# A hybrid-attention encoder layer: keys loaded once with queries turned on chip, value products one group later, and another order of loads and passes in the merge

## The chip, the cores and the metric

The kernel runs on one core of a Trainium2 chip. The metric is the device time of one execution in microseconds (us). The engines of the core are named as in the profile: PE is TensorE (matmuls; PEld is its weight load), DVE is VectorE, ACT is ScalarE, POOL is GpSimd, and SP is SyncE, which here issues nearly all the DMAs. "SPq" marks an instruction of SP's queue that issues a DMA. Each engine works its own queue of instructions in order; semaphores hold an instruction until what it needs is done.

## The reference

One layer on a sequence of 2048 tokens of width 1024, all in float32:

```python
h = rms_norm(x, norm_mix)
q_a, k_a, v_a, q_b, k_b, v_b, g_a, g_b = split(h @ w_in)   # 4352 columns
y_a = windowed_gqa(q_a, k_a, v_a, sink)       # |t-s| <= 128, 8 heads, 2 key/value heads
y_b = neighborhood_attn(q_b, k_b, v_b, rpb)   # 8 heads on a grid of 32 x 64, 8 x 16 neighbours
merged = sigmoid(g_a) * (y_a @ w_proj_a) + sigmoid(g_b) * (y_b @ w_proj_b)
x = x + merged @ w_out
x = x + square(relu(rms_norm(x, norm_mlp) @ w_up)) @ w_down
out = rms_norm(x, norm_final)
```

In the first attention ("A") a block of 128 queries sees the 384 keys around it, with a bias that falls with distance and one sink logit per head. In the second ("B") a tile of queries, 8 grid rows by 16 columns, sees a patch of keys with a learned bias.

## The kernel before, in words

**Arithmetic.** Products of float32 numbers are made from two rounded parts, hi and lo: `a*b = ah*bh + ah*bl + al*bh`, three matmuls (`mm3`, `mm3s`, lines 201 and 278). To split a tile, ACT rounds it (`A.copy`, L275 in `split`) and DVE subtracts (L276). Large products use a seven-product block scheme (Strassen's kind), which is why operands are sums of blocks, numbered 1 to 7.

**Stages, in order of time.** The input projection runs to about 500 us of the span, attention A from there to about 800, attention B to about 1115, the merge (gated projections, then `merged @ w_out`) to about 1390, the up projection to about 1990 and the down projection to the end.

**Scores.** Heads are 64 wide, so hi and lo of a query fill the 128 rows of the array: a query tile is `[qh; ql]`. The keys lie in SBUF twice: plane 0 is `[kh; kl]` and plane 1 is `[kl; kh]`, and the two matmuls of a score (L850 and L851 in A, L1070 in B) use the same query tile against the two planes, which gives all four products. A load of keys is three DMAs: the whole of plane 0 (L830, L1047) and the two halves of plane 1, each on 64 partitions (L831 and L832; L1048 and L1049). In A there are four such loads (`load_kv`), in B eight (`load_k`, one for each head, into two tiles in turn).

**A unit of attention.** There are 32 units of A (`attn_a`) and 32 of B (`attn_b`). A unit loads its queries (L843, L1057), makes scores into PSUM, adds bias and takes the maximum on DVE (L852, L1075), takes the exponential on ACT (L859, L1081) and scales on POOL (L863, L1086). Later it turns the probabilities 128 columns at a time on PE against the identity (L869, L1098); for each group of turned columns ACT rounds them to `ph` (L873, L1104), DVE makes the rest `pl` (L874, L1105), and two sets of matmuls with the values add to a PSUM bank (L875 and L876; L1110). At the end the two halves of the result (values' hi and lo) are added into `ya` or `yb` and stored. `drive` keeps a unit's second part two units behind its first. The values of a unit of B are a DMA of their own (L1060) into one of three tiles.

**Filling.** Beside the attention PE has other work, the gate columns of the projection (`gate_tiles`) and the projection of A's result (`proj_tiles`), dealt out by `paced` between groups of transposes.

**The merge.** It runs twice, for `m` = 0 and 1, each on half the tokens. Eight calls of `gated` load gate values (L1586) and stored projections (L1588) and make the tiles `m0` to `m3`. Then `out_products` makes seven products in the order 1, 2, 5, 6, 3, 7, 4. Each takes its weights from DRAM (`wo_d`, L1487, two loads of 1 MB) and its left operand from the `m` tiles, split by L275 and L276; weights and operands share a ring of six buffers, `pgl`. Beside them, `beside_out` loads rows of `x` (L1562), loads the next part of B's result (`load_y`, L1169), and, in the second pass, prepares the up projection (`up_start`, `up_right`, `up_left_steps`). When a block of rows is finished it is normalised (L230, L241) and turned by DVE (`turned_out`, L253), and goes to DRAM as `h2d` (L257). In the second pass, `turned_last` uses freed `m` tiles for the first of the last two row blocks and `hu` for the last.

**Memory and order.** SBUF is dealt out as stacks of pools from two sides. A pool of a later stage lies where an earlier one lay, and its first writer waits for the earlier one's last user. The order of instructions on each engine isn't that of the program text: a planner simulates the program with its own costs at build and takes, for each engine, what is ready first, with the earlier text preferred. `tc.issue_after(ins)` forbids it to put the instructions of a block ahead of `ins` on that engine's queue; it adds no semaphore. Once built, the order is fixed.

Of the kernel before, what the change touches and what calls it, by code (L numbers as in the profile page):

```python
# [8 lines left out]
F32 = mybir.dt.float32  # L9
# [83 lines left out]
def encoder_layer(ctx, tc, x, norm_mix, w_in, b_gate, sink, rpb, w_pa, w_pb, w_out,  # L93
# [179 lines left out]

    def split(src, hi, lo, eng):
        A.copy(hi, src)  # L275
        return eng.tensor_tensor(out=lo, in0=src, in1=hi.bitcast(F32), op=ALU.subtract).ins  # L276
# [532 lines left out]
    ap_ = pools(s_a, "left", ("dist", "sta", "qa", "ka1", "va1", "ya", "sa", "ph", "pl"), "a")  # L809
# [15 lines left out]
    kas = [T(ap_, [P, 2, S], F32R, f"ka{g}", 1) for g in range(2)]  # L825
    vas = [T(ap_, [P, 16, P], F32R, f"va{g}", 1) for g in range(2)]

    def load_kv(g, m):
        k, kd = kas[g][:, :, m * (S // 2) : (m + 1) * (S // 2)], ks_a[m][g]
        SY.dma_start(k[:, 0].bitcast(F32), kd)  # L830
        SY.dma_start(k[0:64, 1].bitcast(F32), kd[64:128])  # L831
        SY.dma_start(k[64:128, 1].bitcast(F32), kd[0:64])  # L832
        SY.dma_start(vas[g][:, 8 * m : 8 * m + 8].bitcast(F32), vs_a[m][g])

    def attn_a(u, g, i):
# [6 lines left out]
        q = T(ap_, [P, 4, P], F32R, "qa", 3)  # L842
        began.append(SY.dma_start(q.bitcast(F32), qs_a[g][i // 8][:, :, i % 8]).ins)  # L843
# [21 lines left out]
        po = psum("av", 2)  # L865
        for c in range(c0, c1):
# [8 lines left out]
            PE.matmul(po, v[:, i - 1 + c, :], ph, start=c == c0, stop=False)  # L875
            PE.matmul(po, v[:, i - 1 + c, :], pl, start=False, stop=c == c1 - 1)  # L876
        e = u % 2 * 64
        t = (ya if u % 4 < 2 else yb)[e : e + 64]
        A.copy(t, po[64 - e : 128 - e, :])
        V.tensor_tensor(out=t, in0=po[e : e + 64, :], in1=t, op=ALU.add)  # L880
        flush(queue=SY)
        put(y_a[g].rearrange("(h d) t -> d h t", d=64)[:, :, i * P : (i + 1) * P],
            t.rearrange("d (h q) -> d h q", h=4))
# [10 lines left out]
    def drive(units, live, last, ahead=2):  # L894

        for u in units:
            next(u)
            live.append(u)
            if len(live) > ahead:
                next(live.pop(0), None)  # L900
        while last and live:
            next(live.pop(0), None)

# [22 lines left out]
    def gate_tiles(*fs):  # L926
# [33 lines left out]
    def proj_tiles(f):  # L960
# [3 lines left out]
        for b in (0, 2):  # L964
            for i in range(2):
                z = T(wp, [P, 2, BT], F32, "z", 3)
# [20 lines left out]

    live, given = [], [0]
    units_a = [(1, i) for i in range(5)] + [(0, i) for i in range(16)] + [(1, i) for i in range(5, 16)]
    load_kv(1, 0)  # L990
    at = 0
    for n, g, m in ((4, 0, 0), (9, 0, 1), (14, 1, 1)):
        drive((attn_a(u, *units_a[u]) for u in range(at, n)), live, False)
# [4 lines left out]
    drive((attn_a(u, *units_a[u]) for u in range(14, 32)), live, True)  # L998
# [7 lines left out]
    bp = pools(s_b, "right", ("masks", "qb", "braw0", "biass", "stb", "kb0", "biasl", "braw1", "kb1"), "b")  # L1006
# [36 lines left out]
    def load_k(h):  # L1043

        k = T(bp, [P, 2, S], F32R, f"kb{h % 2}", 1)
        kd = ks_b[h // 2][h % 2]
        SY.dma_start(k[:, 0].bitcast(F32), kd)  # L1047
        SY.dma_start(k[0:64, 1].bitcast(F32), kd[64:128])  # L1048
        SY.dma_start(k[64:128, 1].bitcast(F32), kd[0:64])  # L1049
        return k  # L1050

    def attn_b(n_u, h, j, k, bias):
# [3 lines left out]
        q = T(bp, [P, 4, P], F32R, "qb", 3)  # L1056
        SY.dma_start(q.bitcast(F32), qs_b[t][e][:, :, j])  # L1057
        yield
        v = T(bp, [P, 8, P], F32R, f"vb{n_u % 3}", 1)
# [4 lines left out]
        kv = k.rearrange("p z (q f) -> p z q f", q=8)  # L1064
        s = []
        for i in range(4):
            n = B_NR[i] * w
            ps = psum("s", 3)
            for z in range(2):
                PE.matmul(ps[:, :n], q[:, i, :],  # L1070
                          kv[:, z, B_R0[i] // 4 : (B_R0[i] + B_NR[i]) // 4, 4 * B_C0[j] : 4 * (B_C0[j] + w)],
# [16 lines left out]
        flush(queue=SY)  # L1088
        po = psum("av", 2)
        first = True  # L1090
        for pair in range(4):
# [16 lines left out]
            for c, i0, ni, o in pieces:  # L1108
                for z, src in enumerate((ph, pl)):
                    PE.matmul(po[:, i0 * P : (i0 + ni) * P], v[:kp, c, :],  # L1110
                              src[:kp, o : o + ni * P], start=first, stop=(c == 7 and z == 1),
                              skip_group_check=True)
                    first = False

        at = n_u % 2 * 64
        y = yb[at : at + 64]
        A.copy(y, po[64 - at : 128 - at, :])
        V.tensor_tensor(out=y, in0=po[at : at + 64, :], in1=y, op=ALU.add)
        put(y_b[t].rearrange("(e d) (i j t) -> e d i j t", e=2, i=4, j=4)[e, :, :, j, :],
            y.rearrange("d (i t) -> d i t", i=4))  # L1120

    def all_b():
# [3 lines left out]
        for h in range(BH):  # L1126
            k = load_k(h)

            for n, j in enumerate((0, 3, 1, 2) if h == 0 else range(4)):
# [4 lines left out]
                u = attn_b(4 * h + n, h, j, k, bias)  # L1134
                next(u)
                yield u

    def ahead_of(units, n):
        ready = []
        for u in units:  # L1140
            ready.append(u)
            if len(ready) > n:
                yield ready.pop(0)
        yield from ready

# [14 lines left out]
    ring_l = [None]  # L1160
# [679 lines left out]
```

## Time and profile before

| what | us |
|---|---|
| median of 3 runs | 2623.56 |
| lowest and highest of them | 2621.88, 2627.18 |
| the profiled execution, its own time | 2622.45 |
| its span, from the first to the last instruction | 2620.7 |
| PE busy | 2551.7 |
| DVE busy | 1710.1 |
| ACT busy | 1309.0 |
| POOL busy | 354.3 |
| bytes moved | 553.21 MB, 211 GB/s over the span |

A row of the timeline gives the start and length of an instruction in us, its engine and line, what it writes and reads, and in square brackets how long the engine sat idle before it and what ended that idleness. Matmuls are pipelined: 128x512 has a length of 390 ns, but one starts about every 230 ns. A row of the table by stretches gives, for each engine, the busy us and the number of instructions, then the granted clock of PE (1.00 is full speed), the share of the DMA engines and the GB/s.

### The profile page before, as it was taken

What the parts mean: (1) busy time and instruction counts of PE and PEld (TensorE: products, weight loads), DVE (VectorE), ACT (ScalarE), POOL (GpSimd) and SP (SyncE); (2) the same over time, 40 slices, a digit from 0 to 9 for tenths busy, and PEclk for the clock granted to TensorE, in tenths of its full rate; (3) what the DMA queues carried; (4) which work ended last, traced back from release to release, by engine and by line L of the source; (5) the groups of instructions that cost most, each with busy time, mean ns of one, the idle gap of its engine ahead of it and who ended that gap; (6) DMA issues with size and microseconds to landing.
All of it is one profiled execution on the core that took longest, in us unless ns stands there. A gap on an engine that the chain in (4) does not pass through costs nothing.

```text
span 2620.7 us, 34535 instructions
## 1 busy us (share of the span) xinstructions
PE 2551.7 (97%) x11936; PEld 2123.5 (81%) x11936; DVE 1710.1 (65%) x2717; ACT 1309.0 (50%) x2345; POOL 354.3 (14%) x482
## 2 busy tenths in 40 slices
PE   8999999999999999999998999999999999999998
PEld 6788888877787887887877888888887888888887
DVE  8857677657764576665687677766655634554766
ACT  6365565557775675523246554644444332323444
POOL 1001001133446664200000000000000000000011
PEclk9999999999999999999999999999999999999999
DMA  5767878774358998797878665854428825445555
GB/s 185 224 198 251 267 241 278 217 216 113 100 162 196 214 279 231 221 325 267 303 287 251 234 219 191 293 184 145 157 101 298 308 97 185 145 147 167 185 194 168
DMA packets 347695, 553.21 MB, mean 211 GB/s; under 512 B 32072, under 2 KB 152376, under 8 KB 345344
## 3 DMA queue, kind: packets, MB, share of 16 engines
q1 hardware_dynamic: 330336, 510.48, 61.5%
q10 hardware_dynamic: 10944, 24.12, 2.5%
q0 software_dynamic: 6240, 16.40, 2.1%
q8 instruction: 94, 1.54, 0.2%
q14 instruction: 81, 0.66, 0.1%
HBM read 364.17 MB, written 186.71 MB: 210 GB/s over the span
## 4 chain that ended last, share of the span: by engine, by line
PE 75%; DMA 13%; DVE 6%; ACT 3%; SPq 2%; issue 2%; POOL 0%; DVEq 0%; POOLq 0%; ACTq 0%
PE b L280 15%; PE b L279 15%; PE b L281 15%; PE zb L281 5%; PE zb L279 5%; PE zb L280 5%; PE mm L202 2%; PE mm L204 2%; PE mm L203 2%; DMA vb<-vs_b 2%; DMA h2d<-ht 1%; PE av L1110 1%; PE pt L869 1%; DMA z<-zg 1%; PE pt L1098 1%
## 5 line engine op out<-in xcount | busy, mean ns | idle before, releaser
L280 PE MATMUL b<-dwh,dah 128*128 128x512 f32 x896 | 349.2, 390 | 0.4 <-DVE dwh L276 0.4
L281 PE MATMUL b<-dwh,dah 128*128 128x512 f32 x896 | 348.3, 390 | 0.0
L279 PE MATMUL b<-dwh,dah 128*128 128x512 f32 x896 | 339.0, 390 | 1.7 <-ACT dwh L275 1.7
L275 ACT CAST dah<-da 128x1024 fp32r<-128x1024 f32 (+1 forms) x128 | 120.8, 945 | 367.4 <-PE b L281 246.3
L279 PE MATMUL zb<-zh,zwhl 128*128 128x512 f32 x728 | 285.3, 392 | 3.7 <-ACT zc L486 1.3
L280 PE MATMUL zb<-zh,zwhl 128*128 128x512 f32 x728 | 285.6, 392 | 0.0
L281 PE MATMUL zb<-zh,zwhl 128*128 128x512 f32 x728 | 283.9, 391 | 0.8 <-DVE zwhl L276 0.8
L276 DVE TENSOR_TENSOR dah<-da,dah 128x1024 fp32r<-128x1024 f32 (+1 forms) x128 | 139.2, 1090 | 216.1 <-ACT dah L275 213.0
L279 PE MATMUL b<-ubh,uwhlb 128*128 128x512 f32 x592 | 231.5, 392 | 7.7 <-ACT uwhlb L275 4.5
L280 PE MATMUL b<-ubh,uwhlb 128*128 128x512 f32 x592 | 231.7, 391 | 0.5 <-DVE ubh L276 0.5
L281 PE MATMUL b<-ubh,uwhlb 128*128 128x512 f32 x592 | 229.8, 390 | 0.0
L279 PEld LDWEIGHTS b<-dwh,dah 128*128 128x128 f32 x896 | 168.2, 188 | 36.9 <-ACT dwh L275 2.1
L280 PEld LDWEIGHTS b<-dwh,dah 128*128 128x128 f32 x896 | 168.3, 188 | 35.6 <-DVE dwh L276 0.8
L281 PEld LDWEIGHTS b<-dwh,dah 128*128 128x128 f32 x896 | 168.3, 188 | 34.8
L272 DVE TENSOR_TENSOR uc<-b,uc 128x512 f32<-128x512 f32 x160 | 109.3, 689 | 118.1 <-PE b L281 110.8
L279 PEld LDWEIGHTS zb<-zh,zwhl 128*128 128x128 f32 x728 | 137.1, 188 | 34.2 <-ACT zc L486 2.5
L281 PEld LDWEIGHTS zb<-zh,zwhl 128*128 128x128 f32 x728 | 137.1, 188 | 28.9 <-DVE zwhl L276 1.3
L280 PEld LDWEIGHTS zb<-zh,zwhl 128*128 128x128 f32 x728 | 137.1, 188 | 27.7
L202 PE MATMUL mm<-zh,whl 128*128 128x512 f32 x368 | 157.7, 428 | 0.6 <-ACT z L463 0.6
L204 PE MATMUL mm<-zh,whl 128*128 128x512 f32 x368 | 145.5, 395 | 0.0
L203 PE MATMUL mm<-zh,whl 128*128 128x512 f32 x368 | 144.9, 394 | 0.0
L279 PEld LDWEIGHTS b<-ubh,uwhlb 128*128 128x128 f32 x592 | 111.8, 189 | 32.1 <-ACT uwhlb L275 4.9
(262 smaller groups left out, 5694.4 us busy)
## 6 DMA issues: line engine op xcount, KB each, us to landing
at<-uc SPq DMA_DIRECT2D x224, 256.0 KB, 2.1
da<-at SPq DMA_DIRECT2D x96, 512.0 KB, 3.6
dw<-in_w_down_dram SPq DMA_DIRECT2D x160, 256.0 KB, 4.4
uraw<-in_w_up_dram SPq DMA_DIRECT2D x32, 1024.0 KB, 6.0
pgl<-wo_d SPq DMA_DIRECT2D x28, 1024.0 KB, 9.8
zraw<-in_w_in_dram SPq DMA_DIRECT2D x24, 1024.0 KB
z<-zg SPq DMA_DIRECT2D x64, 256.0 KB, 4.3
qs_a<-ze SPq DMA_DIRECT2D x32, 256.0 KB, 6.0
```

Source lines behind the costliest of these rows:

```text
L202: PE.matmul(ps, lh, rh, start=first, stop=False)
L203: PE.matmul(ps, lh, rl, start=False, stop=False)
L204: PE.matmul(ps, ll, rh, start=False, stop=last)
L272: return eng.tensor_tensor(out=out, in0=a, in1=b, op=op).ins
L275: A.copy(hi, src)
L276: return eng.tensor_tensor(out=lo, in0=src, in1=hi.bitcast(F32), op=ALU.subtract).ins
L279: PE.matmul(ps, lh, rh, start=first, stop=False, skip_group_check=True)
L280: PE.matmul(ps, lh, rl, start=False, stop=False, skip_group_check=True)
L281: PE.matmul(ps, ll, rh, start=False, stop=last, skip_group_check=True)
L869: last = PE.transpose(pt[:, h * P : (h + 1) * P], s[:, h, c * P : (c + 1) * P], ident).ins
L1098: last = PE.transpose(pt[:kp, at + (i - i0) * P : at + (i - i0 + 1) * P], s[i][:, rr : rr + kp], ident)
L1110: PE.matmul(po[:, i0 * P : (i0 + ni) * P], v[:kp, c, :], src[:kp, o : o + ni * P], start=first, stop=(c == 7 and z == 1), skip_group_check ...
```

## The change

1. Keys stay once in SBUF, as `[kh; kl]`; each load is one DMA, not three. The query tile gets a second plane: ACT copies the rows 64 to 127 to rows 0 to 63, and DVE the other half (`turn_q`). The two matmuls of a score use the two planes of the query against the same keys.
2. A unit of A, like one of B, has its queries loaded one unit ahead (`ahead_of`), and the turn stands at the head of its scores.
3. The value products of a group are written in the program behind the transposes of the next group, across units too (`behind`, `result`).
4. Pools: `ya` and `va1`, and `qb`, change places; the ring `z` has four buffers, not three.
5. The merge. All four further rows of `x` come behind the loads of the weights then last asked for; so do the next part of B's result, and, in the second pass, all loads of the first four calls of `gated`. `turned_last` uses `m0` and `m1`, not `m2` and `m3`. Two passes of the up projection's right operand (`gained`) are kept behind the last rounding of the left operands so far, and so are the passes for product 3.

```diff
+    rounded = [None]
     def split(src, hi, lo, eng):
-        A.copy(hi, src)
+        rounded[0] = A.copy(hi, src).ins
...
-    ap_ = pools(s_a, "left", ("dist", "sta", "qa", "ka1", "va1", "ya", "sa", "ph", "pl"), "a")
+    ap_ = pools(s_a, "left", ("dist", "sta", "qa", "ka1", "ya", "va1", "sa", "ph", "pl"), "a")
...
+    def load_q(pl, tag, src):
+        q = T(pl, [P, 2, 4, P], F32R, tag, 3)
+        return q, SY.dma_start(q[:, 0].bitcast(F32), src).ins
+
+    def turn_q(q):
+        A.copy(q[0:64, 1], q[64:128, 0].bitcast(F32))
+        V.tensor_copy(out=q[64:128, 1], in_=q[0:64, 0].bitcast(F32))
+
-    kas = [T(ap_, [P, 2, S], F32R, f"ka{g}", 1) for g in range(2)]
+    kas = [T(ap_, [P, S], F32R, f"ka{g}", 1) for g in range(2)]
     def load_kv(g, m):
-        k, kd = kas[g][:, :, m * (S // 2) : (m + 1) * (S // 2)], ks_a[m][g]
-        SY.dma_start(k[:, 0].bitcast(F32), kd)
-        SY.dma_start(k[0:64, 1].bitcast(F32), kd[64:128])
-        SY.dma_start(k[64:128, 1].bitcast(F32), kd[0:64])
+        SY.dma_start(kas[g][:, m * (S // 2) : (m + 1) * (S // 2)].bitcast(F32), ks_a[m][g])
...
-        q = T(ap_, [P, 4, P], F32R, "qa", 3)
-        began.append(SY.dma_start(q.bitcast(F32), qs_a[g][i // 8][:, :, i % 8]).ins)
+        q, ins = load_q(ap_, "qa", qs_a[g][i // 8][:, :, i % 8])
+        began.append(ins)
+        yield
+        turn_q(q)
...
-            PE.matmul(ps[:, :n], q[:, h, :], ka[:, 0, base + lo : base + hi], start=True, stop=False)
-            PE.matmul(ps[:, :n], q[:, h, :], ka[:, 1, base + lo : base + hi], start=False, stop=True)
+            for z in range(2):
+                PE.matmul(ps[:, :n], q[:, z, h, :], ka[:, base + lo : base + hi], start=z == 0, stop=z == 1)
...
+        def result(c, ph, pl):
+            if c == c0:
+                po[0] = psum("av", 2)
+            PE.matmul(po[0], v[:, i - 1 + c, :], ph, start=c == c0, stop=False)
+            PE.matmul(po[0], v[:, i - 1 + c, :], pl, start=False, stop=c == c1 - 1)
+            if c < c1 - 1:
+                return
...
             A.copy(ph, pt)
             V.tensor_tensor(out=pl, in0=pt, in1=ph.bitcast(F32), op=ALU.subtract)
-            PE.matmul(po, v[:, i - 1 + c, :], ph, start=c == c0, stop=False)
-            PE.matmul(po, v[:, i - 1 + c, :], pl, start=False, stop=c == c1 - 1)
...
+            behind(lambda c=c, ph=ph, pl=pl: result(c, ph, pl))
+    lagged = []
+    def behind(f=None):
+        while lagged:
+            lagged.pop(0)()
+        if f:
+            lagged.append(f)
...
-                    zs[f] = T(wp, [P, 2, BT], F32, "z", 3)
+                    zs[f] = T(wp, [P, 2, BT], F32, "z", 4)
...
+    def ahead_of(units, n):
+        ready = []
+        for u in units:
+            next(u)
+            ready.append(u)
+            if len(ready) > n:
+                yield ready.pop(0)
+        yield from ready
...
-    bp = pools(s_b, "right", ("masks", "qb", "braw0", "biass", "stb", "kb0", "biasl", "braw1", "kb1"), "b")
+    bp = pools(s_b, "right", ("masks", "braw0", "biass", "stb", "kb0", "qb", "biasl", "braw1", "kb1"), "b")
...
     def load_k(h):
-        k = T(bp, [P, 2, S], F32R, f"kb{h % 2}", 1)
-        kd = ks_b[h // 2][h % 2]
-        SY.dma_start(k[:, 0].bitcast(F32), kd)
-        SY.dma_start(k[0:64, 1].bitcast(F32), kd[64:128])
-        SY.dma_start(k[64:128, 1].bitcast(F32), kd[0:64])
+        k = T(bp, [P, S], F32R, f"kb{h % 2}", 1)
+        SY.dma_start(k.bitcast(F32), ks_b[h // 2][h % 2])
...
+            behind(lambda pair=pair, pieces=pieces, ph=ph, pl=pl: result(pair, kp, pieces, ph, pl))
...
-                SY.dma_start(raw, y_b[c][:, (2 * m + j) * BT : (2 * m + j + 1) * BT])
+                with tc.issue_after(y_behind[0]) if y_behind[0] else nullcontext():
+                    SY.dma_start(raw, y_b[c][:, (2 * m + j) * BT : (2 * m + j + 1) * BT])
...
         out[4] = parts(a22, V)
+        last_left[0] = rounded[0]
...
-        gained(t, 0)
-        gained(b12, 0)
+        with tc.issue_after(last_left[0]):
+            gained(t, 0)
+            gained(b12, 0)
...
-        parts(3, b22, 1)
+        with tc.issue_after(last_left[0]):
+            parts(3, b22, 1)
...
-            SY.dma_start(w.bitcast(F32), wo_d[n][h].rearrange("k p z c -> p k z c"))
+            wo_dma[0] = SY.dma_start(w.bitcast(F32), wo_d[n][h].rearrange("k p z c -> p k z c")).ins
...
             split(src, t[:, 0], t[:, 1], V)
+            last_left[0] = rounded[0]
...
-            if n < 2:
-                rows[1].extend(x_row(m, 1, 2 * n + t) for t in range(2))
+            if n == 1:
+                with tc.issue_after(wo_dma[0]):
+                    rows[1].extend(x_row(m, 1, t) for t in range(4))
             elif m == 0 and n in (3, 5):
+                y_behind[0] = wo_dma[0]
                 state["y"] = next(loads)
-            elif m == 1:
+            elif m == 1 and n:
                 if n < 5:
                     next(loads)
                 elif n == 6:
-                    free = [T(p4x, [P, 2, 2, BT], F32, f"m{t}", 1).rearrange("p a b c -> p a (b c)") for t in (2, 3)]
+                    free = [T(p4x, [P, 2, 2, BT], F32, f"m{t}", 1).rearrange("p a b c -> p a (b c)") for t in (0, 1)]
                     turned_last(0, lambda g: free[g // 2][:, g % 2])
...
         def gated(f):
+            with tc.issue_after(wo_dma[0]) if m and f < 4 else nullcontext():
+                gated_at(f)
+        def gated_at(f):
```

The unit of B is changed like that of A; its `result` takes the pieces of a pair of chunks and ends the unit at the fourth pair.

More of the change, by code (lines that the diff above doesn't have):

```diff
@@ L997, in encoder_layer @@
     paced(fill, given, 84, 92, 12)
[L998 removed]
+    drive(all_a, live, True)
     paced(fill, given, 84, 92, 12, last=True)
@@ L1107, in attn_b @@
                 pieces.reverse()
[L1108 to L1120, printed above, removed]
+            behind(lambda pair=pair, pieces=pieces, ph=ph, pl=pl: result(pair, kp, pieces, ph, pl))
     def all_b():
```

71 lines of the change are left out of this document (41 added, 30 removed).

## The prediction

> **What bounds the kernel now.** I read the page first, then the stretches, then PE's idle moments one by one in the timeline, and last what SP and ACT did just before each.
>
> ```profile
> span 2620.7 us, 34535 instructions
> PE 2551.7 (97%) x11936; PEld 2123.5 (81%) x11936; DVE 1710.1 (65%) x2717; ACT 1309.0 (50%) x2345; POOL 354.3 (14%) x482
> ...
> core 0: us, PE busy (x) PEld busy (x) DVE busy (x) ACT busy (x) POOL busy (x), PEclk, DMA share, GB/s
> 500.00:1450.00 950.00, 907.19 (x4656) 764.98 (x4655) 623.18 (x1315) 523.46 (x1185) 298.31 (x390) 0.99 0.76 226
> 1450.00:2621.00 1171.00, 1159.04 (x5110) 959.23 (x5108) 727.08 (x942) 510.78 (x758) 14.59 (x17) 1.00 0.56 189
> ...
> 800.00:840.00 40.00, 34.19 (x184) 29.58 (x183) 17.84 (x49) 19.56 (x48) 20.59 (x25) 0.91 1.00 217
> 1034.00:1048.00 14.00, 13.64 (x72) 12.42 (x73) 7.64 (x18) 7.27 (x17) 5.64 (x6) 0.79 0.69 207
> 1195.00:1240.00 45.00, 42.78 (x182) 35.36 (x183) 24.46 (x33) 14.57 (x23) 1.67 (x3) 0.96 0.67 249
> 1285.00:1330.00 45.00, 41.58 (x176) 33.64 (x175) 36.01 (x47) 16.92 (x27) 0.00 (x0) 0.96 1.05 395
> 1410.00:1450.00 40.00, 35.65 (x148) 29.33 (x149) 29.70 (x35) 21.87 (x34) 0.00 (x0) 0.91 0.74 265
> ```
>
> PE bounds it, at 97%. The change leaves PE's work as it is: the same matmuls of the same shapes, and each had its own weight load before (as many PEld as PE). So only PE's idle time and slow clock can be won. All edits lie between 500 and 1450 us, where PE is idle for 950.00 - 907.19 = 42.8 us. The five stretches below that row show the clock granted short of 1.00; the loss is length times shortfall: 3.6, 2.9, 1.8, 1.8 and 3.6, together 13.7 us. The most that can be won is about 56 us. The idle time lies in a few places:
>
> ```profile
> 822.77 0.73 PE L1070 MATMUL s<-kb,qb 128*128 128x288 f32 x3 [2.19 <-DMA kb<-ks_b]
> 829.29 2.68 PE L1070 MATMUL s<-kb,qb 128*128 128x384 f32 x6 [3.02 <-DMA qb<-qs_b]
> 1034.36 0.55 PE L1110 MATMUL av<-phb,vb 96*128 96x256 f32 x1 [3.74 <-DMA vb<-vs_b]
> 1197.22 0.76 PE L279 MATMUL b<-pgl,pgl 128*128 128x512 f32 x1 [4.21 <-DMA pgl<-wo_d]
> 1322.28 0.50 PE L279 MATMUL b<-pgl,pgl 128*128 128x512 f32 x1 [3.42 <-ACT pgl L275]
> 1392.45 0.73 PE L279 MATMUL b<-ubh,uwhlb 128*128 128x512 f32 x2 [1.59 <-ACT ubh L275]
> 1414.35 0.79 PE L279 MATMUL b<-ubh,uwhlb 128*128 128x512 f32 x1 [4.48 <-ACT uwhlb L275]
> ...
> PE av L1110 <- DVE plb L1105: 4.8, 10, 1.0
> PE s L1070 <- DVE stb L1075: 1.6, 2, 1.2
> PE av L1110 <- ACT phb L1104: 2.3, 4, 0.9
> PE av L875 <- ACT ph L873: 2.1, 3, 1.1
> PE av L876 <- DVE pl L874: 1.4, 5, 0.4
> ```
>
> Seven gaps hold 22.7 us, three from loads in B, four in the merge; the waits of value products for `ph` and `pl` hold 4.8 + 2.3 + 2.1 + 1.4 = 10.6 us in 22 pieces. After a long gap PE is also slow: the scores at 829.29 took 2.68 us for six. The Trainium skill ("TensorE: Matmul & The Clock Gate", Part 1) has the clock halved after an idle window of about 3.4 us. By that rule the gaps of 2.19 and 3.02 us would cost no clock and the sum below would be 3.6 us smaller; the trace, with 0.91 granted between 800 and 840, does not agree.
>
> **Keys once (edit 1, the loads).**
>
> ```profile
> 804.91 17.73 DMA kb<-ks_b
> ...
> 823.28 5.87 DMA qb<-qs_b
> ...
> qb<-qs_b SPq DMA_DIRECT2D x32, 256.0 KB, 6.4
> kb<-ks_b SPq DMA_DIRECT2D x8, 1024.0 KB, 11.3
> kb<-ks_b SPq DMA_DIRECT2D x16, 512.0 KB, 12.8
> ...
> 1013.12 0.91 SPq L1047 DMA_DIRECT2D kb<-ks_b  x1
> ...
> 1019.11 0.58 SPq L1060 DMA_DIRECT2D vb<-vs_b  x1
> ```
>
> B loses 16 DMAs of 512 KB, 8 MB, where the DMA share is 1.00 (800 to 840); A loses eight smaller ones, which no gap above waits for. At 804.91 the last third of the second head's keys is issued and lands 17.73 us later, at 822.64; PE had run dry 2.19 us before, at 820.6. Half the bytes land in about half the time, near 814, before PE runs dry; the queries issued at 823.28, behind those keys on SP's queue, come forward as well. That is 2.19 + 3.02 + 3.6 of clock = 8.8 us. At 1019.11 values are issued behind 2 MB of keys (from 1013.12) and PE gets them at 1034.36; without 1 MB of those at the 207 GB/s of the row from 1034, they land 1 MB / 207 GB/s = 5 us sooner, more than the 3.74 us gap. That is 3.74 + 2.9 = 6.6 us. Together 15.4; the low end is a third, 5, if other transfers take the room. I take 12, near the upper end, since both gaps follow a load that is halved. Next late would be values again, whose slot is freed by the unit three before.
>
> **The turn (edits 1 and 2).**
>
> ```profile
> L1117 ACT COPY yb<-av 64x512 f32<-64x512 f32 x32 | 18.6, 581 | 27.9 <-DMA y_b<-yb 11.8 <-PE av L1110 6.6 <-DMA zp<-z 5.0
> L243 DVE TENSOR_SCALAR xin<-xin,st 128x1024 f32<-128x1024 f32 x4 | 3.0, 751 | 1.1 <-POOL st L234 1.1
> ```
>
> 64 turns: ACT 64 x 0.58 = 37 us; DVE 64 x 0.75/2 = 24 us (half the columns of L243's row). ACT is busy 523 and DVE 623 of the 950 us, so both have room, and the filling work of PE covers it. The new wait is one of PE's first score matmul, and of ACT and DVE for the queries' DMA: behind it on ACT stand roundings of `ph`, behind it on DVE those of `pl`, for which PE's value products wait. Lower end 0. Upper end 37 us, were each ACT copy on the path. The nearest row is the roundings: 22 late ones of about 220, 0.48 us each; for 64 turns that gives 64/220 x 10.6 = 3.1. I take 3. The Trainium skill ("SBUF — State Buffer", Who interferes with whom) says that a copy in DVE's two-port mode and a POOL instruction shut each other out for a whole instruction. No run here shows that; by it DVE's turn could wait out one of POOL's scalings, and the sum would be some 2 us larger.
>
> **The lag (edit 3).** It moves 10.6 us of waits behind at least one more group of transposes. Ends 0 (the planner had filled these places as well as it could) and 10.6. I take 7, since the waits are short (at most 1.1 us, less than a group with its six filling matmuls, which start 0.23 us apart). Next late: the values' slots are freed a group later, so their loads start later. A's and B's score waits for DVE stay.
>
> **Pools and ring (edit 4).** They move no work; a wrong neighbour would show as a load waiting for an old tile. I cost them at nothing: what hides it is the lead of one unit for queries; if gone, each costs a gap like that at 829.29.
>
> **The merge (edit 5).**
>
> ```profile
> 1179.66 4.44 SPq L1169 DMA_DIRECT2D yraw<-y_b  x4
> 1184.27 0.98 SPq L1588 DMA_DIRECT2D z<-zp  x2
> ...
> 1189.86 4.06 SPq L1487 DMA_DIRECT2D pgl<-wo_d  x4
> ...
> 1318.14 1.94 ACT L1285 ACTIVATE uraw<-uraw,g_mix 128x512 f32<-128x512 f32 x3
> ...
> 1321.20 1.98 ACT L275 CAST pgl<-m 128x1024 fp32r<-128x1024 f32 x2
> ...
> 1391.35 2.00 ACT L275 CAST ubh<-uraw 128x1024 fp32r<-128x1024 f32 x2 [2.67 <-DMA h2d<-m]
> ...
> 1407.38 1.96 ACT L546 ACTIVATE ubh<-uraw,g_mix 128x512 fp32r<-128x512 f32 x3 [2.77 <-DMA h2d<-hu]
> ...
> 1413.27 1.03 ACT L275 CAST uwhlb<-uraw 128x1024 fp32r<-128x1024 f32 x1
> ```
>
> Gap at 1197: the weights are issued at 1189.86, behind four loads of `y_b` and loads of the second pass's `gated`. Both now go behind weights: up to 4.21 + 1.8 of clock. Gap at 1322: on ACT passes of `gained` (L1285) stand ahead of the rounding of `pgl` at 1321.20; they now follow the last such rounding: up to 3.42 + 1.8. They land in ACT's later idle time (8 x 0.65 = 5.2 us). Gap at 1392: ACT waits 2.67 us for the stores from `m` before it may write `ubh`, which lies there; with `m0` and `m1` freed earlier and another neighbour, 1.59. Gap at 1414: ACT waits 2.77 us for stores from `hu` and then does product 3's passes, ahead of the rounding that PE needs (1413.27); these now stand behind it: 4.48 + 3.6. Sum 20.9. Upper end that; lower end 6, if only the last gap's idle and a part of its clock are won. I take 17, since at each gap the instruction that stood in front is the one that is moved. The price is that the second pass's first loads start only after the last weights of the first: behind them on SP stand gate values, for which DVE and then PE wait; the cover is the products still to run then.
>
> **Sum.** 12 + 7 - 3 + 17 = 33. A new order on every queue will bring a wait or two that aren't there now; I allow 6 us, one gap like those seen with its clock. Net 27. The profiled execution took 2622.45 us (span 2620.7, 1.75 around it; the median is 2623.56, 1.1 more): 2622.45 - 27 = 2595.
>
> **Rivals.**
> *Late queries stop two engines (slower).* A query tile that lands late now holds ACT and DVE, not PE alone. For: 6.4 us to landing in the middle, and one late tile at 829.29. Against: 31 of 32 came in time, and DMA gets 8 MB less. Each costs 3.02 us and half of the clock loss that two gaps share there (3.6 / 2), 4.8 in all; from six on (27 / 4.8) the gain is gone, and eight make 2595 + 8 x 4.8 = 2633.
> *The lag and the keys win little.* The planner had already put filling work there, and a slot of values freed later makes a new values gap (3.74 + 2.9). Then 5 + 0 - 3 + 17 - 6 - 6.6 = 6: 2616.
> *The merge only moves its stalls.* The second pass starts late and the loads of `x` collide with weights (395 GB/s at 1285 to 1330). Then 12 + 7 - 3 + 6 - 6 = 16: 2606.
> *It doesn't do what it says.* The planner puts the moved pieces where they were, and only the turn is new: 2622.
>
> **How the numbers follow.** My forecast 0.55 (its own range 2575 to 2605), the merge's stalls 0.17, lag and keys 0.12, nothing done 0.06, late queries 0.10. 0.2% is 5 us, about what a measurement can tell from no change. Faster: 0.55 + 0.17 + 0.09 of lag and keys = 0.81; same: the other 0.03 and 0.04 of nothing done = 0.07; slower: late queries and the last 0.02 = 0.12. The range starts at all of the upper ends, 15.4 + 10.6 + 20.9 = 47, so 2575, and ends past the unchanged time, at 2626, which leaves out late queries and little else.
>
> **What would show it.** Right: no PE gap over 1 us ended by kb, qb or vb, or by `pgl` and `uwhlb`; the granted clock at 0.98 or more in the five stretches; 8 MB fewer moved in B. The lag: waits for `ph` and `pl` under 4 us in sum. Wrong: PE waits at scores ended by the turn, with ACT or DVE idle for qb; gaps at the first products of the merge's second pass; longer waits for vb.

## The result, and the profile after

The changed kernel takes 2682.12 us (median of 4 runs, 2678.34 to 2687.74) against 2622.72 us for the kernel before in the same session. The ratio is 1.0225, with a 95% interval of 1.0203 to 1.0247: it is 2.2% slower, about 59 us, where 27 us less were predicted. The profiled execution, the slowest of the four, took 2687.74 us with a span of 2686.0.

The head of the page of the changed kernel, in the order of the one before:

```profile
span 2686.0 us, 34629 instructions
...
PE 2574.7 (96%) x11936; PEld 2128.8 (79%) x11936; DVE 1743.1 (65%) x2781; ACT 1351.5 (50%) x2409; POOL 355.8 (13%) x482
...
DMA packets 345776, 542.73 MB, mean 202 GB/s; under 512 B 31688, under 2 KB 151992, under 8 KB 344448
```

The matmuls are the same 11936. The span grew by 2686.0 - 2620.7 = 65.3 us. PE is busy 2574.7 - 2551.7 = 23.0 us longer with the same work, and idle 42.3 us longer. Part of the 23.0 is slower clock: the mean granted clock of the span is 0.987 in place of 0.994, and by the profile's record of the granted clock PE works at half clock for 51 us in place of 22, which makes some 14 us. The rest stays open. ACT and DVE got their 64 copies each and still have plenty of idle time. 10.5 MB less are moved. None of these totals says why the kernel is slower. The next view, by stretches, says where: the first table is of the changed kernel, A and B together and then the merge and the up projection, the second is of the kernel before. The stretches are bounded, within a few us, by the first scores of A, the first products of the merge and the first of the down projection; the first stretch holds 14 matmuls more in the changed kernel, some 3 us.

```profile
536.00:1183.00 647.00, 585.77 (x3169) 490.59 (x3168) 411.58 (x1041) 415.59 (x1024) 284.92 (x372) 0.97 0.54 159
1183.00:2068.00 885.00, 861.68 (x3757) 709.69 (x3756) 600.03 (x768) 421.43 (x610) 9.79 (x16) 0.99 0.65 225
```

```profile
539.00:1125.00 586.00, 560.12 (x3155) 480.73 (x3156) 377.10 (x974) 374.33 (x959) 279.66 (x364) 0.99 0.71 190
1125.00:2002.00 877.00, 859.05 (x3757) 708.28 (x3755) 600.08 (x770) 419.54 (x609) 9.77 (x16) 0.99 0.66 228
```

A and B took 586 us and now take 647, with PE idle 61 us in place of 26 and the clock at 0.97 in place of 0.99. The merge and what follows take 8 us more, where 17 less were predicted. Who waits in A and B is told by the waits of the changed kernel (engine, tile and line that waits, what ended the wait; us in total, times, longest):

```profile
ACT qb L834 <- DMA qb<-qs_b: 55.5, 28, 5.5
DVE qb L835 <- DMA qb<-qs_b: 54.7, 26, 5.6
DVE qa L835 <- DMA qa<-qs_a: 46.6, 27, 5.8
ACT qa L834 <- DMA qa<-qs_a: 20.3, 12, 4.0
...
PE s L1107 <- DVE stb L1112: 12.1, 8, 3.6
PE s L862 <- DVE sta L863: 10.1, 8, 6.5
PE av L882 <- DVE pl L901: 9.1, 12, 3.2
PE av L1133 <- DVE plb L1160: 7.7, 13, 2.2
PE av L881 <- ACT ph L900: 6.8, 7, 1.8
```

L834 and L835 are the two halves of the turn. In 93 of 128 cases (28 + 26 + 27 + 12) the half stood at the head of its engine's queue before its queries had landed, and the engine stood still: 177 us in all. No such rows exist in the profile before. PE itself hardly waits for the turn. It waits for what stands behind the turn: the passes over scores that free a bank (`sta`, `stb`) and the rounding of probabilities. One such place in the timeline:

```profile
982.39 0.56 SPq L830 DMA_DIRECT2D qb<-qs_b  x1
...
990.09 0.62 ACT L834 CAST qb<-qb 64x512 fp32r<-64x512 f32 x1 [3.01 <-DMA qb<-qs_b]
...
990.09 0.42 DVE L835 CAST qb<-qb 64x512 fp32r<-64x512 f32 x1 [5.59 <-DMA qb<-qs_b]
990.54 0.18 DVE L1120 RECIPROCAL stb<-stb 128x4 f32<-128x4 f32 x1
...
991.09 0.55 DVE L1160 TENSOR_TENSOR plb<-pt,phb 128x384 fp32r<-128x384 f32 x1
...
991.23 1.01 PE L1107 MATMUL s<-kb,qb 128*128 128x384 f32 x2 [3.62 <-DVE stb L1112]
```

The load is issued at 982.39, and both halves of its turn start at 990.09, when it has landed. DVE waits 5.59 us for it. A reciprocal and a subtraction that were ready, and the passes that free the score banks, stand behind, and PE runs dry for 3.62 us. And these queries weren't wanted yet: when the 32 loads, turns and sets of eight score matmuls of B are matched in their order in the timeline, DVE's half begins 4.8 us (median, never over 7.7) after the issue of its load, and the unit's scores begin about 18 us after that. In A it is 3.2 and about 13 us. (The queries of B's first three units are loaded and turned at the start of A already.) The planner put the turn right behind its load, and not ahead of its use.

### The profile page after: what moved, and what is told of

The parts are those of the page before. It is cut to its first block, busy times and chain, and to the rows that moved or that the text cites. A ratio compares the mean times of both kernels' runs of the same rounds, so it can differ in the third digit from the quotient of the medians.

```text
span 2686.0 us, 34629 instructions
## 1 busy us (share of the span) xinstructions
PE 2574.7 (96%) x11936; PEld 2128.8 (79%) x11936; DVE 1743.1 (65%) x2781; ACT 1351.5 (50%) x2409; POOL 355.8 (13%) x482
## 4 chain that ended last, share of the span: by engine, by line
PE 73%; DMA 11%; DVE 7%; ACT 4%; issue 3%; SPq 1%; POOL 0%; ACTq 0%; DVEq 0%; POOLq 0%
PE b L283 15%; PE b L282 15%; PE b L281 15%; PE zb L281 4%; PE zb L283 4%; PE zb L282 4%; DMA qb<-qs_b 4%; PE mm L202 2%; DMA qa<-qs_a 2%; PE mm L203 2%; PE mm L204 2%; PE av L1133 1%; PE b L202 1%; PE b L203 1%; PE b L204 1%
## 5 line engine op out<-in xcount | busy, mean ns | idle before, releaser
L202 PE MATMUL mm<-zh,whl 128*128 128x512 f32 x368 | 159.5, 434 | 10.9 <-DVE z L1007 6.4
L203 PE MATMUL mm<-zh,whl 128*128 128x512 f32 x368 | 147.5, 401 | 0.0
L204 PE MATMUL mm<-zh,whl 128*128 128x512 f32 x368 | 147.3, 400 | 0.0
```

The lines of the kernel that those rows point to most:

```text
L202: PE.matmul(ps, lh, rh, start=first, stop=False)
L203: PE.matmul(ps, lh, rl, start=False, stop=False)
L204: PE.matmul(ps, ll, rh, start=False, stop=last)
```

## The experiments

Theory T: the turn costs time by its place in the queues of ACT and DVE; the late loads hold these engines, and everything behind. Its rivals: W, the work of the 128 copies costs it; L, the lead of one unit is too short; and that the lag did it (R1 in the texts below) or that the loss is spread over the parts (R2).

**The edits apart.** Edits 1, 2 and 4 alone (keys, turn, pools):

> The kernel before with keys once, the turn, the lead of a unit and the new pools and ring alone (edits 1, 2 and 4). Theory T: the planner puts each turn directly behind its query load, the load takes longer than it was planned with, and ACT and DVE stand still before 54 of the 64 turns or so; those stalls are the whole loss of A and B, some 60 us. T expects 2670 to 2690, with ACT and DVE waits for qa and qb of over 100 us in sum. Rival R1: the lag makes the loss, by what it holds longer. R1 expects 2605 to 2630 here. Rival R2: the loss is spread over the parts. R2 expects 2635 to 2655.

```diff
 (the changed kernel, with edits 3 and 5 taken back)
-            behind(lambda c=c, ph=ph, pl=pl: result(c, ph, pl))
+            PE.matmul(po, v[:, i - 1 + c, :], ph, start=c == c0, stop=False)
+            PE.matmul(po, v[:, i - 1 + c, :], pl, start=False, stop=c == c1 - 1)
...
```

Measured: 2673.53 us, ratio 1.0182 (1.0161 to 1.0203). Its waits of the turn for the loads are 50.1 + 50.6 + 15.6 + 41.5 = 158 us. So four fifths of the loss (48 of 59 us) come with these edits.

Edit 3 alone (the lag):

> The kernel before with the lag of the value products alone (edit 3). T expects 2612 to 2625, PE's waits for ph and pl under 6 us in place of 10.6. R1 expects 2670 or more. R2 expects 2630 to 2645.

```diff
 (the kernel before, with)
-            PE.matmul(po, v[:, i - 1 + c, :], ph, start=c == c0, stop=False)
-            PE.matmul(po, v[:, i - 1 + c, :], pl, start=False, stop=c == c1 - 1)
+            behind(lambda c=c, ph=ph, pl=pl: result(c, ph, pl))
...
```

Measured: 2620.27 us, ratio 0.9989 (0.9975 to 1.0003). A gain of some 3 us, not told apart from none.

Edit 5 alone (the merge):

> The kernel before with the merge's order of loads and passes alone (edit 5; the ring z keeps three buffers). In the changed kernel the stages from the first product of the merge to the first of the down projection took 7 us longer than before. If that is edit 5's own, this takes 2627 to 2633. If edit 5 does what the prediction said and what spoils it comes from the planner's other order upstream, it takes 2605 to 2615.

```diff
 (the kernel before, with)
-        A.copy(hi, src)
+        rounded[0] = A.copy(hi, src).ins
...
 (and the order of loads and passes of edit 5)
```

Measured: 2627.93 us, ratio 1.0013 (0.9999 to 1.0027). Of the four gaps that were to go, the one for `wo_d` (4.21 us) and the one for `uwhlb` (4.48) are gone. Those for `pgl` and `ubh` are still there in another form: 2.61 us for the low part of `pgl`, and 3.73 and 3.12 for `ubh`. And two new ones came. PE's rows with their idle time, in the merge of this kernel:

```profile
1252.90 0.50 PE L202 MATMUL b<-pgr,whl 128*128 128x512 f32 x1 [2.97 <-DVE xr L272]
...
1346.23 0.77 PE L281 MATMUL b<-pgl,pgl 128*128 128x512 f32 x1 [5.58 <-issue]
```

The first is at the first products of the second pass. What stands before it on ACT and SP:

```profile
1250.51 0.63 ACT L230 ACTIVATE junk<-xr 128x512 bf16<-128x512 f32 x1 [8.42 <-DMA z<-zg]
...
1242.91 0.98 SPq L189 DMA_DIRECT2D raw<-in_w_proj_b_dram  x2
1244.18 1.02 SPq L1601 DMA_DIRECT2D z<-zg  x2
```

Gate values `z` are still being issued at 1244.18, behind the weights, as edit 5 orders; ACT stands idle for 8.42 us, which the profile puts down to them, then DVE empties the banks (`xr`), then PE goes on. It looks like the price that the prediction named for this edit ("behind them on SP stand gate values, for which DVE and then PE wait") and then costed at nothing; no run moves these loads alone. The cause of the second gap, 5.58 us with nothing that the profile shows, stays open; a like gap is in each profile with the new merge (3.9 to 6.0 us), and in none with the old.

Edits 3 and 5 together, without keys and turn:

> The changed kernel without edits 1, 2 and 4: keys twice, no turn, old pools and ring, with the lag and the merge's order. T expects 2605 to 2630, A and B as long as before. R1 expects 2670 or more. R2 expects 2635 to 2655.

```diff
 (the kernel before, with the diffs of the last two)
```

Measured: 2626.61 us, ratio 1.0005 (0.9991 to 1.0018). Without the keys and the turn nothing of the loss is left that can be told. The last fifth, between the run with edits 1, 2 and 4 and the changed kernel, is hardly clear of noise (their intervals touch at 1.0203), and no run says what it is.

**The turn at another place or on another engine.** Held behind the last unit's last exponential (ACT) and reciprocal (DVE):

> The changed kernel with each unit's turn kept behind the last exponential (on ACT) and the reciprocal (on DVE) of the unit before, so that the planner can't put it directly behind its load. The work is the same. T (the place of the turn in the queues costs the time, not the turn's work): waits of ACT and DVE for qa and qb fall from 177 us to under 40, and the time to 2615 to 2640. Rival W (the turn's own work, 33 us of ACT and 27 of DVE, is what delays the casts): no change, 2665 to 2690.

```diff
     def turn_q(q):
-        A.copy(q[0:64, 1], q[64:128, 0].bitcast(F32))
-        V.tensor_copy(out=q[64:128, 1], in_=q[0:64, 0].bitcast(F32))
+        with tc.issue_after(held[0]) if held[0] else nullcontext(), tc.issue_after(held[1]) if held[1] else nullcontext():
+            A.copy(q[0:64, 1], q[64:128, 0].bitcast(F32))
+            V.tensor_copy(out=q[64:128, 1], in_=q[0:64, 0].bitcast(F32))
... (held[0] and held[1] are set at each unit's last exponential and reciprocal)
```

Measured: 2674.97 us, ratio 1.0188 (1.0171 to 1.0205). T's number missed by 35 us. The waits of this kernel show that one wait took the other's place:

```profile
PE s L865 <- DVE qa L838: 19.6, 17, 1.9
PE s L1111 <- DVE stb L1116: 7.8, 7, 4.4
PE s L1111 <- DVE qb L838: 7.4, 7, 1.9
...
ACT qa L837 <- DMA qa<-qs_a: 4.0, 1, 4.0
...
DVE qa L838 <- DMA qa<-qs_a: 3.3, 1, 3.3
```

The waits for loads fell from 177 to 7.3 us. But now PE's scores wait for the turn (19.6 + 7.4 us, 24 times): a unit's scores can't start until the softmax of the unit before is through on both engines. This run alone would have spoken for W.

A lead of two units, with rings of four query tiles:

> The changed kernel with queries loaded two units ahead, in rings of four. Rival L (a lead of one unit is too short, so queries are late): waits for qa and qb fall to under 60 us, and the time to 2620 to 2645. T: the planner puts the turn behind its load whatever the lead, so the waits stay over 120 us, and the time at 2660 to 2690.

```diff
-        q = T(pl, [P, 2, 4, P], F32R, tag, 3)
+        q = T(pl, [P, 2, 4, P], F32R, tag, 4)
...
-    all_a = ahead_of((attn_a(u, *units_a[u]) for u in range(32)), 1)
+    all_a = ahead_of((attn_a(u, *units_a[u]) for u in range(32)), 2)
...
-    units = ahead_of(all_b(), 1)
+    units = ahead_of(all_b(), 2)
```

Measured: 2684.32 us, ratio 1.0232 (1.0216 to 1.0247), and 169 us of waits for the loads. L falls: the load goes out earlier, the turn follows it, and the engines wait as before.

Both halves on POOL:

> The changed kernel with both halves of the turn on POOL, ACT and DVE free of it. T: POOL stands still for the queries in their place; since POOL is busy 31% of A and B and scales the probabilities two units ahead of their use, the time falls to 2620 to 2650. W: the same. If the wait for queries by whatever engine is what counts, 2665 or more.

```diff
-        A.copy(q[0:64, 1], q[64:128, 0].bitcast(F32))
-        V.tensor_copy(out=q[64:128, 1], in_=q[0:64, 0].bitcast(F32))
+        G.tensor_copy(out=q[0:64, 1], in_=q[64:128, 0].bitcast(F32))
+        G.tensor_copy(out=q[64:128, 1], in_=q[0:64, 0].bitcast(F32))
```

Measured: 2619.78 us, ratio 0.9987 (0.9978 to 0.9997). POOL's waits in this kernel:

```profile
POOL qb L834 <- DMA qb<-qs_b: 55.4, 17, 6.9
POOL qa L834 <- DMA qa<-qs_a: 47.1, 12, 14.4
```

POOL now stands still for 102.5 us for the same loads. (It is busier than was expected, too: 284.92 of 647 us in A and B of the changed kernel, 44% and not 31%.) The time shows nothing of it: 0.9987 / 0.9975 is 3 us over the kernel that has no turn at all (next run), and the two intervals overlap. So a wait for these loads costs next to nothing on an engine that PE needs nothing from soon.

The second plane by two more DMAs, no turn at all:

> The changed kernel with the second plane of each query tile brought by two further DMAs of 128 KB (64 x 2, 16 MB more, in place of the 10 MB that the keys no longer take), and no turn on ACT and DVE. T and W: the loss of A and B goes, 2615 to 2635. If the loss came from keys once, the lead or the pools, it stays at 2670 or more.

```diff
+        SY.dma_start(q[0:64, 1].bitcast(F32), src[64:128])
+        SY.dma_start(q[64:128, 1].bitcast(F32), src[0:64])
         return q, SY.dma_start(q[:, 0].bitcast(F32), src).ins
...
     def turn_q(q):
-        A.copy(q[0:64, 1], q[64:128, 0].bitcast(F32))
-        V.tensor_copy(out=q[64:128, 1], in_=q[0:64, 0].bitcast(F32))
+        pass
```

Measured: 2619.03 us, ratio 0.9975 (0.9966 to 0.9985). Against it the changed kernel is 1.0225 / 0.9975 = 1.025, about 66 us: that is what the turn on ACT and DVE costs. This kernel also has the new pools and ring (edit 4) and the lead of a unit, and is no slower than the kernel before, so these cost little, if anything.

**Work and wait apart.** The runs so far took away work and wait together. The next two add only one of them to the kernel with the second plane by DMA. First the work alone, on a tile that is always there:

> The kernel that loads the second plane by DMA (2619.0 us), and beside it ACT and DVE copy 64x512 numbers per unit as the turn did, but from a tile of zeros that is always there into a spare tile that nobody reads. The turn's work without its waits. Theory T: 2617 to 2627, since both engines have room. Rival W: 2660 or more.

```diff
     def turn_q(q):
-        pass
+        A.copy(spare[1][0:64], spare[0][64:128])
+        V.tensor_copy(out=spare[1][64:128], in_=spare[0][0:64])
... (and the two spare tiles, made once in A and once in B)
```

Measured: 2629.86 us, ratio 1.0033 (1.0021 to 1.0044), a little over T's range and 30 us under W's. Over the kernel without a turn that is 11 us by the medians and 15 by the two ratios. Two rows of its timeline, DVE and PE:

```profile
803.06 9.68 DVE L846 CAST spare<-spare 64x512 fp32r<-64x512 f32 x12
...
814.83 0.58 PE L1145 MATMUL av<-plb,vb 96*128 96x256 f32 x1 [6.47 <-DVE plb L1172]
```

With nothing to wait for, the planner put twelve copies in a row, and the subtraction behind them came too late for PE. The gap of 6.47 us and the slow clock after it (0.50 from 810.8 to 821, where PE is busy for 6.17 us, so some 3 us) come to 9.6 us, most of what this kernel loses. So the work of a spread turn may cost less.

Then the wait alone, with copies of 8 columns that nobody needs:

> The kernel that loads the second plane by DMA (2619.0 us), and beside it ACT and DVE copy 64x8 numbers per unit from the query tile into a spare tile that nobody reads: the turn's waits for the load without its work, and PE waits for none of it. Theory T: 100 us or more of waits for qa and qb on ACT and DVE, time 2655 to 2685. Rival W: within 2615 to 2627.

```diff
     def turn_q(q):
-        pass
+        A.copy(spare[1][0:64, 0:8], q[64:128, 0, 0, 0:8].bitcast(F32))
+        V.tensor_copy(out=spare[1][64:128, 0:8], in_=q[0:64, 0, 0, 0:8].bitcast(F32))
... (and the spare tiles)
```

Measured: 2686.04 us, ratio 1.0250 (1.0235 to 1.0266). Its waits, of DVE and ACT:

```profile
DVE spare L846 <- DMA qb<-qs_b: 74.0, 26, 8.2
DVE spare L846 <- DMA qa<-qs_a: 48.9, 27, 5.7
...
ACT spare L845 <- DMA qb<-qs_b: 48.5, 17, 7.3
ACT spare L845 <- DMA qa<-qs_a: 17.8, 9, 5.3
```

128 tiny copies, whose results nobody reads, cost as much as the whole turn: 189 us of waits on two engines with half their time or a third of it idle, and 1.0250 / 0.9975 = 1.028 in time over the kernel without them, about 72 us. With the work alone at 11 to 15 us, that settles T against W. (The two aren't parts of a sum: together they come to more than the 66 us of the turn.)

The real turn, one unit earlier than in the held kernel, behind the softmax of the unit before the last:

> The changed kernel with each turn kept behind the exponentials (ACT) and the reciprocal (DVE) of the unit before the last, one unit earlier than in the kernel held behind the last one's. Theory T (the turn costs time by where it stands in ACT's and DVE's queues: too early it holds them for the load, too late it holds the scores): waits of the turns for the loads under 20 us in sum, score waits for the turn under 5 us, time 2615 to 2632. Rival W (the turn's work on ACT and DVE costs it, wherever it stands): 2660 or more.

```diff
+    exps, recs = [], []
     def turn_q(q):
-        A.copy(q[0:64, 1], q[64:128, 0].bitcast(F32))
-        V.tensor_copy(out=q[64:128, 1], in_=q[0:64, 0].bitcast(F32))
+        with tc.issue_after(exps[-2]) if len(exps) > 1 else nullcontext(), tc.issue_after(recs[-2]) if len(recs) > 1 else nullcontext():
+            A.copy(q[0:64, 1], q[64:128, 0].bitcast(F32))
+            V.tensor_copy(out=q[64:128, 1], in_=q[0:64, 0].bitcast(F32))
... (each unit's last exponential and reciprocal are added to exps and recs)
```

Measured: 2631.31 us, ratio 1.0042 (1.0027 to 1.0057). Its waits:

```profile
ACT qa L837 <- DMA qa<-qs_a: 4.4, 2, 4.1
DVE qa L838 <- DMA qa<-qs_a: 4.4, 2, 3.4
PE s L1112 <- DVE stb L1117: 4.3, 4, 1.8
PE av L887 <- DVE pl L906: 3.5, 7, 1.2
```

8.8 us of waits for loads, and no wait of scores for the turn of note. The same instructions, moved by a unit, win 1.0225 / 1.0042 = 1.018, about 48 us, over the changed kernel: T holds, with a place that is neither too early nor too late.

**What the turn costs at a better place.** The last kernel is still 12 us above the one without a turn by the medians, and 18 by the two ratios (1.0042 / 0.9975). Three theories were put to it: X, DVE's copies and POOL's instructions hold each other up; Y, ACT's half holds the roundings behind it; Z, either engine is alike. Both halves on ACT, and both on DVE, at that same place:

> The kernel with the turn kept behind the unit before the last (2631.3 us, some 12 us above the one that loads the second plane by DMA), with both halves of the turn on ACT. Theory X (DVE's copies and POOL's instructions hold each other up: in that kernel 16 of the 64 copies took 0.5 to 2.0 us in place of 0.42, 10.0 us in sum, all of them beside a POOL instruction): the time falls to 2617 to 2626. Rival Y (ACT's half costs it: the roundings of the probabilities stand behind it): 2638 or more. Rival Z (either engine, alike): 2627 to 2636.

```diff
             A.copy(q[0:64, 1], q[64:128, 0].bitcast(F32))
-            V.tensor_copy(out=q[64:128, 1], in_=q[0:64, 0].bitcast(F32))
+            A.copy(q[64:128, 1], q[0:64, 0].bitcast(F32))
```

> The same with both halves on DVE. Theory X: more copies of over 0.5 us, 20 us of excess in sum, and 2636 to 2650. Rival Y: 2617 to 2626. Rival Z: 2627 to 2636.

```diff
-            A.copy(q[0:64, 1], q[64:128, 0].bitcast(F32))
+            V.tensor_copy(out=q[0:64, 1], in_=q[64:128, 0].bitcast(F32))
             V.tensor_copy(out=q[64:128, 1], in_=q[0:64, 0].bitcast(F32))
```

Measured: on ACT 2650.56 us, ratio 1.0099 (1.0082 to 1.0116); on DVE 2648.25 us, ratio 1.0095 (1.0080 to 1.0110). None of the three theories has both: X is right on DVE and wrong on ACT, Y the other way round, Z wrong on both. On DVE the sign of X is there too: 80 of its 128 halves took longer than 0.47 us, 33.6 us over 0.42 each in sum. Either engine, given both halves, is worse than each given one. On DVE the waits of value products for its subtraction in B doubled, from 7.9 to 16.8 us; on ACT those in A for the rounding went from 1.6 to 6.6 us. So at a good place the work itself isn't free, on either engine; how the 12 to 18 us split stays open.

**A kernel that beats both.** Keys once, the second plane by DMA, the lag, and the old merge:

> Keys once, second query plane by DMA, the lag, and the merge as it was before. If the merge's new order costs what it did alone and with the lag (5 to 6 us), this takes 2611 to 2616, against 2619.0 with the new merge; if the merge's order costs nothing once the stages before it are quick, 2617 to 2621.

```diff
 (the kernel with the second plane by DMA, with edit 5 taken back)
```

Measured: 2612.46 us, ratio 0.9967 (0.9956 to 0.9978), 8.7 us faster than the kernel before, and 68 us faster than the changed one by the two ratios. Its page:

```profile
span 2610.9 us, 34710 instructions
...
PE 2547.7 (98%) x11936; PEld 2118.9 (81%) x11936; DVE 1711.4 (66%) x2717; ACT 1310.1 (50%) x2345; POOL 354.8 (14%) x482
...
DMA packets 380592, 559.51 MB, mean 214 GB/s; under 512 B 33736, under 2 KB 186808, under 8 KB 379264
```

It moves more bytes than the kernel before (559.51 MB against 553.21) and is faster, by a third of a percent.

## Why the prediction was wrong

**Keys once: right in kind, half in size.** The gaps for `kb` are gone, and of the changed kernel's gaps over 1 us in B none is ended by `kb`, `qb` or `vb`. Its price is read without the turn: the best kernel against the lag alone is 0.9967 / 0.9989 = 0.9978, some 6 us, give or take 5, with the queries' second plane loaded by DMA and the lead of a unit as well; 12 were taken, 5 to 15.4 were the ends.

**The turn: the step that failed.** It was taken at 3 us and measured about 66, over its upper end of 37. Three things went wrong in it. The work was bounded well (0.62 and 0.42 us a half, where 0.58 and 0.375 were taken). The wait was taken from "22 late ones of about 220", the roundings that PE waited for; those follow PE's own work and were no likeness of an instruction that waits for a DMA. And "31 of 32 came in time" was said of scores on PE, which come late; a turn is late or not by where the planner puts it, and it was put right behind its load. "What hides it is the lead of one unit for queries" holds for PE's scores: the queries were there about 18 us ahead of them in B. It doesn't hold for two engines that work in order and had taken up the wait at once. The rival *Late queries stop two engines* had the mechanism, with ACT and DVE held rather than PE, and was given 0.10. It was priced at eight late tiles, 2633; there were 93 late halves, and 2682. Its sign in the profile ("PE waits at scores ended by the turn, with ACT or DVE idle for qb") is there by half: the engines are idle for `qb`, but PE waits for what stands behind the turn.

**The lag: too large.** Taken at 7, measured at about 3 (0.9989), within what can't be told from none. In the kernel with the lag alone the waits of value products for `plb`, `ph` and `pl` still come to 3.6 + 2.1 + 1.3 = 7.0 us, so under 4 us of 10.6 went. In the changed kernel the same waits, for which the prediction had "under 4 us in sum" as a sign, are 9.1 + 7.7 + 6.8 + 3.4 = 27.0 us, where the kernel with the second plane by DMA has 4.4 + 2.0 + 1.3 = 7.7.

**The merge: wrong sign.** Taken at a gain of 17, measured at 0.0013, a loss of 3 us that is hardly told from none. The rival *The merge only moves its stalls* was right, its price of 6 us gained was not. The sign that the prediction gave for being right, no gap over 1 us ended by `pgl` or `uwhlb`, holds in the changed kernel and says nothing of the time, since other gaps came. The lines of the changed kernel, where the two gaps of the merge alone come back:

```profile
1312.79 0.80 PE L202 MATMUL b<-pgr,whl 128*128 128x512 f32 x1 [4.76 <-DVE xr L272]
...
1406.50 0.76 PE L281 MATMUL b<-pgl,pgl 128*128 128x512 f32 x1 [5.58 <-issue]
...
1470.55 0.79 PE L282 MATMUL b<-ubh,uwhlb 128*128 128x512 f32 x1 [3.35 <-DVE ubh L278]
```

The third is for `ubh`, where the prediction meant to win 1.59 us. The first is the sign that the prediction gave for being wrong, "gaps at the first products of the merge's second pass". The step that failed is "since at each gap the instruction that stood in front is the one that is moved": true, and no proof that nothing else comes to stand there.

**The sum.** The allowance of 6 us for new waits was meant for one gap. The four terms measured give -6 - 3 + 66 + 3 = 60, against the 59 measured. That is no check of the terms: the ratios for keys, lag and turn are taken along one chain of kernels from the one before to the changed one, which leaves only the merge to differ (0.0013 alone, 0.9975 / 0.9967 - 1 = 0.0008 in the chain).

## What to carry to other kernels

In these runs an instruction that waited for a DMA held up all that stood behind it on its engine, however small it was (128 copies of under 0.2 us as a rule cost some 72 us) and however idle the engine was on average. Before such an instruction is put on an engine with work that PE wants soon, ask where in the queue the scheduler will put it, not when its result is needed; then hold it there by hand, or give it to an engine with nothing urgent behind it, or to the DMA itself. If holding it doesn't help, look at the waits again before dropping the theory: too late looks, by its time, just like too early.

## What the hardware showed that was not expected

The clock. PE was busy 23.0 us longer for the same matmuls, though in B only one of its gaps was over 3.4 us (3.62, the one shown at 991.23). The granted clock in the trace is 1.00 or 0.50 and nothing between, and it is 0.50 in pieces of 3.41 us or twice or three times that. A piece is as long as the idle window of about 3.4 us that the Trainium skill ("TensorE: Matmul & The Clock Gate", Part 1) gives; but taken as one gap of that length it would let B lose clock at that one gap at most, and the trace has six drops in B. What goes with a drop is how long PE sat idle in the piece before, in however many gaps. Two pairs of pieces that follow each other (start and end, length, PE busy, granted clock):

```profile
1020.88:1024.29 3.41, 0.97 (x4) 1.00 0.48 178
1024.29:1027.70 3.41, 3.41 (x14) 0.50 0.70 198
...
962.80:966.20 3.40, 1.80 (x11) 1.00 1.05 385
966.20:969.60 3.40, 3.28 (x19) 1.00 0.82 252
```

In the first pair PE is idle 2.44 us of 3.41, and the next piece has half the clock; in the second it is idle 1.60, and the clock stays. So it is throughout the changed kernel: its 13 drops follow pieces with 1.71 to 2.94 us of idle time, and the some 740 pieces that no drop follows have 1.66 us at most. In the kernel before it is the same, with drops from 2.01 us on (the one at 828.28, behind the gaps of 2.19 and 3.02 us that the prediction read) and none up to 1.65. The drop at 1061.80 follows 1.71 us of idle time in which no single gap is over 1 us. In the other runs some drops and some stays lie between 0.85 and 1.88 us, so about half a piece is as close as these traces say. Between 500 and 1500 us the clock is at half for 64.9 us in the changed kernel and for 27.3 in the one before.

DVE and POOL. The prediction said that no run showed the rule of the Trainium skill ("SBUF — State Buffer", Who interferes with whom) by which a DVE copy in its two-port mode and a POOL instruction shut each other out. The changed kernel agrees with it. Two of DVE's halves, with the POOL rows beside them:

```profile
928.91 4.00 DVE L835 CAST qb<-qb 64x512 fp32r<-64x512 f32 x1 [0.71 <-DMA qb<-qs_b]
...
1019.53 3.02 DVE L835 CAST qb<-qb 64x512 fp32r<-64x512 f32 x1 [1.28 <-DMA qb<-qs_b]
...
927.26 2.41 POOL L179 TENSOR_TENSOR whl<-raw,whl 128x1024 fp32r<-128x1024 f32 x1
929.61 3.00 POOL L1078 TENSOR_TENSOR biass<-braw,masks 128x288 f32<-128x288 f32 x3
...
1019.24 3.02 POOL L1078 TENSOR_TENSOR biass<-braw,masks 128x288 f32<-128x288 f32 x3
```

Copies of 0.42 us took 4.00 and 3.02, and ended 0.3 us after POOL's group did (932.91 against 932.61, 1022.55 against 1022.26). Of the 64 halves on DVE, 15 were longer than 0.47 us, all of them beside a POOL instruction, and 11.2 us over 0.42 each in sum; the 44 with no POOL instruction beside them were not, nor were five that ran beside one. In the kernel with the turn one unit earlier the order decides: the 18 longer halves all began while a POOL instruction ran, and of the 38 that began before the POOL instruction beside them none was longer. The prediction put the rule at some 2 us. In the kernel with the work alone the excess is 8.3 us, so this part of the loss lies within the 11 to 15 us of that kernel. That POOL is the cause was not tested by itself.
